# A retention projection by seven block products in place of eight, with its gate's columns ahead of it

## The chip, the cores and the metric

The kernel runs on one core of one Trainium2 chip. The metric is the device time of one execution in microseconds (us); lower is better. A core has five engines that run side by side: TensorE (PE, matmuls into PSUM banks), VectorE (DVE), ScalarE (ACT), GpSimd (POOL, which also issues some transfers) and SyncE (SP, which issues most transfers). Transfers (DMA) run on 16 shared DMA engines.

## The reference

One inference step of a hybrid backbone with one layer, on 128 context tokens and 512 latent tokens. In the part that matters here, the normalised input `h` goes through an input projection; attention gives `ya`, retention gives `yr`, each is projected to 1024 channels, gated, summed and projected again:

```python
def token_mixer(h, ...):
    z = h @ w_in
    q, k, v, rq, rk, rv, rg, ga, gr = jnp.split(z, ...)
    ...
    ya = attend_blocks(q, k_all, v_all)
    yr, s_f, s_b = retention_branch(rq, rk, rv, rg, ...)
    y = jax.nn.sigmoid(ga) * (ya @ w_att_o) + jax.nn.sigmoid(gr) * (yr @ w_ret_o)
    return y @ w_out, (k, v, s_f, s_b)
```

Then come a gated residual add, a second modulated norm, a gated MLP with a width-3 convolution, a second residual add and a last norm. All matrices are float32; `w_ret_o` is 1024 x 1024.

## The kernel before, in words

All 640 tokens (context first, then latent) are handled together, in `NT` = 5 tiles of 128 or in two halves of `HALF` = 320. The 1024 channels are `KD` = 8 rows of 128.

Every float32 matmul operand is split into a high part (a rounding to the type fp32r) and a low part (the rest), and a product is three matmuls: high x high, high x low, low x high. ScalarE makes the high part of a weight by a cast, VectorE the low part by a subtraction (`load_w`, `w_split`). In some places the low part is made by a negated copy on ScalarE and an accumulating transfer that POOL issues. Raw weights come in loads of 1 MB into one of two `raw` buffers; split weights lie in eight `wh` slots of 1024 columns.

There are two matmul helpers. `b_col` makes one column of 128 output channels, transposed (channels on partitions, tokens along the row): for each token half a PSUM bank takes 8 k x 3 matmuls of 128x320, then an evacuation function is called. `a_group` makes 512 output channels for five token tiles, with the activations as the stationary operand: a first round over channels rows 0 to 3 for all tiles, then rows 4 to 7.

The stages around the change, in order:

1. Attention. Its gate columns (`ga`) are left as tanh values in eight tiles `tha` of pool `f1`.
2. The attention projection (`w_att_o`, eight `b_col`); `ya_ev` (L786) multiplies each column with its gate in place. Rows of the modulation matrix `w_mod` are loaded and used in between (`mod_rest`, L254).
3. Retention, whose outputs lie in `rvv` (pool `f0`).
4. The retention projection. `yr_blocks` transposes `rvv` by TensorE into `yrT`, high and low part (L992, L643, L644). `gr_col` makes a column of the retention gate (tanh, L1004), `ret_col` a column of `yr @ w_ret_o`, whose evacuation multiplies by the gate (L1014), adds `tha` (L1015) and splits the sum (`yhi` by ScalarE, L1018; `ylo` by POOL, L1019). Two gate columns come first, beside the transposes; then retention and gate columns alternate.
5. `gate_rows` (L272, L274) spreads the residual gate over the partitions, in tile `gb`.
6. The output projection: `a_group` over the first 512 columns of `w_out` with `evac_out` (L1076 to L1078), then the other 512 tile by tile (`out_half`), followed two tiles behind by `h2_trans`, which writes the second norm's transposed output, split, into `h2`. The buffers of `h2` held the first norm's output `hT` until the last gate column had read it. `h2` has a zero column between context and latent tokens and at the end, for the convolution.
7. The MLP. Its up-projection, but for the first columns, already goes by units of seven block products (`unit_group`, L1343 to L1414): two output columns of 128 by two token halves with the 1024 channels in two halves would be eight block products; sums of weight blocks and of activation blocks make it seven (Strassen's scheme in Winograd's form), each of 4 k x 3 matmuls (L1384 to L1387).

Outside blocks marked `tc.manual_schedule` a planner orders the instructions of each engine before the run, by estimated times; inside a marked block the named engines keep the order of the program. Each engine and each queue then works strictly in its order. A tile that takes the place of a closed pool's tile waits until the last reader of that one is done.

Of the kernel before, what the change touches and what calls it, by code (L numbers as in the profile page):

```python
# [69 lines left out]
def hybrid_step(ctx: ExitStack, tc: tile.TileContext, a: dict, o: dict):  # L70
# [708 lines left out]

    for c in range(KD):  # L780
# [199 lines left out]
    gbp = Pool("gate", side="right")  # L980
    gb = gbp([P, 2, DM])
    yrp = Pool("yr", side="right")
    yrT = [yrp([P, KD, TOK], F32R) for _ in range(2)]
    yrTk = [[x[:, k] for k in range(KD)] for x in yrT]
    rt = Pool("rt", side="right")

# [10 lines left out]
    thr = {}  # L997

    def gr_col(c, w):
        thr[c] = rt([P, TOK], tag="thr", bufs=2)  # L1000
        cc = slice((c % 2) * P, (c % 2 + 1) * P)

        def ev(hf, ts, ps):
            nc.scalar.activation(thr[c][:, ts], ps, AF.Tanh, scale=0.5)  # L1004
        yield from b_col(w, cc, hTk, mm, ev)

    yhi, ylo = {}, {}

    def ret_col(c, w):
        cc = slice((c % 2) * P, (c % 2 + 1) * P)  # L1010

        def ev(hf, ts, ps):
            v = thr[c][:, ts]
            V.scalar_tensor_tensor(v, v, 1.0, ps, op0=ALU.add, op1=ALU.mult)  # L1014
            V.tensor_add(v, v, tha[c][:, ts])  # L1015
            if hf:
                yhi[c] = f1(F32R)
                nc.scalar.copy(yhi[c], thr[c])  # L1018
                nc.gpsimd.tensor_sub(ylo[c], thr[c], yhi[c].bitcast(F32))  # L1019
        yield from b_col(w, cc, yrTk, mm, ev)  # L1020

    def wgr(c):
        return load_w(w_in[:, O_GR + c * P:O_GR + (c + 2) * P], 8, 256)

    yb = yr_blocks()
    wg = wgr(0)
    for c in range(2):
        for _ in gr_col(c, wg):
            next(yb, None)
    run(yb)  # L1030
    ylo4 = [f0(F32R) for _ in range(2)]
    ylo = {c: ylo4[c // 4][:, c % 4] for c in range(KD)}
    for c in range(0, KD, 2):
        wr = load_w(a["w_ret_o"][0, :, c * P:(c + 2) * P], 8, 256)
        if c + 2 < KD:
            wg = wgr(c + 2)
        for j in range(2):
            run(ret_col(c + j, wr))
            if c + 2 < KD:
                run(gr_col(c + 2 + j, wg))  # L1040
# [549 lines left out]
```

## Time and profile before

| | |
|---|---|
| median of 3 runs | 1184.67 us (1184.38 to 1185.37) |
| the profiled execution's own time | 1184.71 us |
| its span in the profile | 1182.9 us |
| granted TensorE clock | 0.998 |
| busy: TensorE / VectorE / ScalarE / POOL | 1153.6 / 738.3 / 567.1 / 175.9 us |
| moved by DMA | 139.02 MB, mean 118 GB/s |

The profile comes from one execution. Its page gives the busy time of each engine, the chain of work that ended last, and groups of instructions by line. Queries of the trace give single instructions in order of time ("start, duration, engine, line, operation, output<-inputs, shapes"), the busy time of each engine in a stretch ("stretch, length, PE busy (count) PEld busy (count) DVE ACT POOL, granted clock, DMA share, GB/s"), and transfers with their size and the time from issue to landing. Matmuls are pipelined: the time from one start to the next is what a matmul costs, not its listed duration.

### The profile page before, as it was taken

Reading aid. Unit: us, or ns where it says so; the run is one execution under the profiler, and the core shown is the slowest. Engines: PE = TensorE matmul, PEld = TensorE weight load, DVE = VectorE, ACT = ScalarE, POOL = GpSimd, SP = SyncE. Lnnn points to the kernel's source line nnn. Section 1 sums busy time; section 2 is a strip of 40 time slices with the busy share of each in tenths; the row PEclk is TensorE's granted clock in tenths of the full one; section 3 lists DMA queues with packets and bytes.
Section 4 is the critical chain, followed back from the end, with each engine's and each line's share of the span. In section 5 each row is a group of like instructions: output and inputs, shape, how many; then the busy total and the mean of one; then the engine's idle time right before and its main releaser. Section 6 shows DMA issues by size and latency. Waiting matters only on the chain.

```text
span 1182.9 us, 18329 instructions
## 1 busy us (share of the span) xinstructions
PE 1153.6 (98%) x7317; PEld 1038.8 (88%) x7317; DVE 738.3 (62%) x1419; ACT 567.1 (48%) x1019; POOL 175.9 (15%) x177
## 2 busy tenths in 40 slices
PE   4999999999999999999999999999999999999996
PEld 4788899999988888888999988999989999899995
DVE  4566977665234436453333339969767688598887
ACT  4355656552132224443222335558657556565473
POOL 0042200000012100033011122011112111121113
PEclk9999999999999999999999999999999999999999
DMA  8742111115554431112122539445666657556543
GB/s 283 250 145 71 37 36 37 36 46 171 213 187 171 153 98 45 36 37 71 36 72 72 180 109 167 111 91 107 158 134 130 142 137 172 125 112 149 141 112 120
DMA packets 130917, 139.02 MB, mean 118 GB/s; under 512 B 26240, under 2 KB 98000, under 8 KB 130832
## 3 DMA queue, kind: packets, MB, share of 16 engines
q1 hardware_dynamic: 106592, 112.95, 29.4%
q0 software_dynamic: 24240, 24.91, 13.8%
q8 instruction: 57, 0.93, 0.3%
q14 instruction: 28, 0.23, 0.1%
HBM read 110.32 MB, written 6.03 MB: 98 GB/s over the span
## 4 chain that ended last, share of the span: by engine, by line
PE 88%; DVE 4%; issue 3%; DMA 2%; POOL 1%; ACT 1%; SPq 0%; DVEq 0%; POOLq 0%; ACTq 0%
DMA t7.u5.5_6930<-in_conv_w 1%; POOL x1.u1.1_6376 L1077 1%; POOL f0.s.5_3520 L941 0%; DVE acts.u2.2_97 L1105 0%; DMA xin.u1.1_108<-in_x_sample 0%; DMA x1.u1.1_6376<-in_x_prompt 0%; DVE acts.u1.1_96 L1104 0%; DVE acts.u2.2_97 L412 0%; PE mm1.mm.11_300 L159 0%; PE mm7.mm.9_7496 L1387 0%; PE mm7.mm.45_9650 L1384 0%; PE mm7.mm.33_8918 L1384 0%; PE mm7.mm.57_10402 L1384 0%; PE mm7.mm.54_10133 L1384 0%; PE mm7.mm.42_9401 L1384 0%
## 5 line engine op out<-in xcount | busy, mean ns | idle before, releaser
L830 POOL TENSOR_TENSOR ret.r2k.6_3630<-ret.u5.5_3523,ret.u1.1_3516 128x256 f32<-128x256 f32 x2 | 1.4, 740 | 205.0 <-ACT ret.u5.5_3523 L826 205.0
L1398 DVE TENSOR_TENSOR t7.u4.4_6925<-t7.u4.4_6925,const.u1.1_70 128x322 f32<-128x322 f32 x10 | 5.0, 496 | 11.6 <-ACT const.u1.1_70 L1397 11.6
L879 DVE SCALAR_TENSOR_TENSOR ret2.u1.1_4317<-ret2.u1.1_4317,const.u13.13_93 64x128 f32<-64x128 f32 x24 | 6.8, 339 | 6.6 <-ACT ret2.u1.1_4317 L872 6.5
L150 DVE TENSOR_TENSOR weights.wh.183_6565<-weights.raw.181_6562,weights.wh.182_6564 128x1024 fp32r<-128x1024 f32 x1 | 1.2, 1224 | 14.3 <-ACT weights.wh.182_6564 L145 14.3
L1309 POOL TENSOR_TENSOR x1.u1.1_6376<-x1.u1.1_6376,weights.raw.410_10987 128x512 f32<-128x512 f32 x5 | 8.2, 1637 | 10.3 <-ACT x1.tm.112_11000 L1281 7.5
L881 DVE SCALAR_TENSOR_TENSOR ret2.u1.1_4317<-ret2.u1.1_4317,const.u13.13_93 64x128 f32<-64x128 f32 x24 | 6.6, 383 | 4.8 <-ACT ret2.u1.1_4317 L874 4.8
L832 DVE TENSOR_TENSOR ret.u5.5_3523<-ret.u5.5_3523,ret.u1.1_3516 128x512 f32<-128x512 f32 x5 | 3.5, 692 | 9.4 <-POOL ret.r2k.8_3701 L830 3.3
L832 DVE TENSOR_TENSOR ret.u4.4_3522<-ret.u4.4_3522,ret.u1.1_3516 128x512 f32<-128x512 f32 x5 | 3.5, 693 | 9.0 <-POOL ret.r2k.11_3881 L830 4.7
L409 ACT CAST acts.u1.1_96<-f0.s.1_109 128x640 fp32r<-128x640 f32 x4 | 2.9, 727 | 11.2 <-DVE f0.s.1_109 L407 11.2
L562 POOL TENSOR_TENSOR p1.u1.1_609<-p1.u3.3_613,p1q.u1.1_603 128x512 f32<-128x512 f32 x1 | 1.3, 1310 | 45.6 <-DMA p1.vc.6_618<-in_cache_v 45.6
L409 ACT CAST acts.u1.1_96<-f0.s.2_110 128x640 fp32r<-128x640 f32 x4 | 2.9, 729 | 10.1 <-DVE f0.s.2_110 L407 10.1
L371 PE MATMUL mm1.mm.1_167<-const.u1.1_70,xin.u1.1_108 128*128 128x128 f32 x4 | 1.1, 435 | 6.8 <-DVE xin.u1.1_108 L362 6.8
L150 DVE TENSOR_TENSOR weights.wh.108_4347<-weights.raw.106_4344,weights.wh.107_4346 128x1024 fp32r<-128x1024 f32 x1 | 1.2, 1226 | 10.3 <-ACT weights.wh.107_4346 L145 10.3
L145 ACT CAST weights.wh.112_4502<-weights.raw.111_4500 128x1024 fp32r<-128x1024 f32 x1 | 1.1, 1050 | 13.3 <-PE mm3.mm.36_4215 L158 13.3
L941 POOL TENSOR_TENSOR f0.s.5_3520<-f0.s.5_3520,ret2.ny20.11_4899 128x512 f32<-128x512 f32 x5 | 6.0, 1235 | 9.1 <-DVE ret2.ny20.11_4899 L217 9.1
L868 POOL DMA_DIRECT2D out_new_state_ret_fwd<-ret.r2k.25_4340 x1 | 0.7, 676 | 43.8 <-ACT ret.r2k.25_4340 L867 43.8
L531 ACT ACTIVATE f0.s.3_715<-f0.s.3_715,p1q.ny20.11_883 128x128 f32<-128x128 f32 x20 | 6.0, 388 | 2.5 <-DVE p1q.ny20.11_883 L215 2.5
L257 DVE COPY mod2.wr.9_4307<-aux3.aux.15_4274 128x128 f32<-128x128 f32 x1 | 0.3, 291 | 10.9 <-PE aux3.aux.15_4274 L254 10.9
L371 PEld LDWEIGHTS mm1.mm.1_167<-const.u1.1_70,xin.u1.1_108 128*128 128x128 f32 x4 | 0.7, 217 | 7.0 <-DVE xin.u1.1_108 L362 7.0
L1275 DVE TENSOR_TENSOR x1.u1.1_6376<-x1.u1.1_6376,gate.u1.1_5306 128x512 f32<-128x512 f32 x10 | 6.8, 685 | 0.0
L145 ACT CAST weights.wh.182_6564<-weights.raw.181_6562 128x1024 fp32r<-128x1024 f32 x1 | 1.1, 1055 | 11.5 <-PE mm3.mm.83_6396 L158 11.5
L145 ACT CAST weights.wh.77_3609<-weights.raw.76_3607 128x1024 fp32r<-128x1024 f32 x1 | 1.0, 1045 | 11.5 <-PE mm3.mm.16_3447 L193 11.5
(7028 smaller groups left out, 4881.6 us busy)
## 6 DMA issues: line engine op xcount, KB each, us to landing
spill.u1.1_6384<-x1.u1.1_6376 POOLq DMA_DIRECT2D x5, 512.0 KB, 4.3
xin.u1.1_108<-in_x_sample SPq DMA_DIRECT2D x4, 512.0 KB
p0.u5.5_125<-in_w_mod SPq DMA_DIRECT2D x2, 1024.0 KB
p0.u6.6_131<-in_w_mod SPq DMA_DIRECT2D x2, 1024.0 KB
p0.u7.7_134<-in_w_mod SPq DMA_DIRECT2D x2, 1024.0 KB
mod.wm.6_2916<-in_w_mod SPq DMA_DIRECT2D x1, 2048.0 KB
mod.wm.8_3067<-in_w_mod SPq DMA_DIRECT2D x1, 2048.0 KB
mod.wm.10_3222<-in_w_mod SPq DMA_DIRECT2D x1, 2048.0 KB
```

Of the source, the lines that this page charges most:

```text
L145: nc.scalar.copy(hi, rv)
L150: (lo_eng or V).tensor_sub(lo, rv, hi.bitcast(F32))
L409: nc.scalar.copy(hT[0][:, k, :], xk)
L531: nc.scalar.activation(x[:, j], x[:, j], AF.Copy, scale=rstd[:, j:j + 1])
L832: V.tensor_mul(z, z, r1[:, t, 0:1, :].to_broadcast([P, 8, 64]))
L879: V.scalar_tensor_tensor(Ss[0:64, hh, st + 1, j], Ss[0:64, hh, st, j], cdsel[0:64, h:h + 1], Ss[0:64, hh, st + 1, j], op0=ALU.mult, op1=AL ...
L881: V.scalar_tensor_tensor(Ss[64:128, hh, 2 - st, j], Ss[64:128, hh, 3 - st, j], cdsel[64:128, h:h + 1], Ss[64:128, hh, 2 - st, j], op0=ALU. ...
L941: nc.gpsimd.tensor_mul(ov, ov, rso[:, 4 * t:4 * t + 4].unsqueeze(2).to_broadcast([P, 4, P]))
L1077: (V if g else nc.gpsimd).tensor_add(x1[:, t, gs], x1[:, t, gs], tm)
L1275: V.tensor_mul(x1[:, t, gs], x1[:, t, gs], gb[:, t == 0, gs])
L1309: eng.tensor_mul(x, x, fg[:, c0:c0 + 512])
L1398: V.tensor_sub(u[1][:, hi_u], u[1][:, hi_u], u3[i])
```

## The change

The retention projection takes the form that the MLP's up-projection has. In detail:

- All eight gate columns come first and stay in one tile `thr` of 8 x 640. The transposes of `yr_blocks` go two to a step beside them.
- `ret_sums` makes three sums of activation blocks and a fourth kept as a product operand, each split; its scratch is the part of `thr` that belongs to columns 6 and 7.
- Four units (`ret_unit`), each for two output columns, do seven products of 4 k x 3 matmuls of 128x320. `prep` makes the weight sums and their split; in two of the seven the low part comes by an accumulating transfer. The products keep the program's order on TensorE; the last product of a unit is done two products into the next.
- Each finished column is multiplied by its gate, and the attention branch's column is added by an accumulating transfer from DRAM. For that, `ya_ev` has written each column of `tha` to DRAM (`thd`).
- The merged column is split straight into `h2`, with the layout of the second norm (a gap after the context tokens), so `a_group` and `out_half` read it with an offset of one for the latent tokens.
- `gate_rows` follows the last product in the same ordered block, and `gb` is allocated after the retention operands are released.

```diff
-    def a_group(w, act, mm, evac, lo_eng=None):
+    def a_group(w, act, mm, evac, lo_eng=None, gap=0):
...
-                ts = slice(t * P, (t + 1) * P)
+                ts = slice(t * P + gap * (t > 0), (t + 1) * P + gap * (t > 0))
...
+    x1d = dp([P, NT, DM])
+    thd = dp([P, KD, TOK])
...
             V.scalar_tensor_tensor(tha[c][:, ts], tha[c][:, ts], 1.0, ps, op0=ALU.add, op1=ALU.mult)
+            if hf:
+                nc.gpsimd.dma_start(thd[:, c, :], tha[c])
...
+    thr = rt([P, KD, TOK])
...
+    def ret_sums():
...
+        x = thr[:, 6:8, :].rearrange("p a b -> p (a b)").rearrange("p (k t) -> p k t", k=4)
...
+        def diff(xs, zs):
+            V.tensor_sub(x, xs[0], zs[0])
+            V.tensor_add(x, x, xs[1])
+            V.tensor_sub(x, x, zs[1])
+
+        def neg_sum(zs):
+            V.scalar_tensor_tensor(x, x, -1.0, zs[0], op0=ALU.mult, op1=ALU.subtract)
+            V.tensor_sub(x, x, zs[1])
+
+        for m, fn in ((3, lambda: diff(q[0, 0], q[1, 0])), (1, lambda: diff(q[1, 1], q[1, 0])),
+                      (2, lambda: neg_sum(q[0, 0])), (4, lambda: neg_sum(q[0, 1]))):
+            fn()
+            nc.scalar.copy(ys[m][0], x)
+            V.tensor_sub(ys[m][1], x, ys[m][0].bitcast(F32))
+
+    for c in range(KD):
...
+        def gr_ev(hf, ts, ps, c=c):
+            nc.scalar.activation(thr[:, c, ts], ps, AF.Tanh, scale=0.5)
+        for _ in b_col(wg, slice((c % 2) * P, (c % 2 + 1) * P), hTk, mm, gr_ev):
+            for _ in range(2):
+                next(yb, None)
+        if c == 1:
+            run(yb)
+            ret_sums()
+
+    def ret_unit(p):
...
+        def prep(m):
+            at, add = PLAN[m]
+            src = bs[at]
+            if add:
+                V.tensor_add(src, src, bs[add])
+            t_ = wp([P, 1024], F32R, tag="wh", bufs=8)
...
+            nc.scalar.copy(hi, src)
+            if m in (2, 3):
+                nc.scalar.activation(lo, src, AF.Copy, scale=-1.0)
+                nc.gpsimd.dma_start(lo, src, accum_op=ALU.add)
+            else:
+                V.tensor_sub(lo, src, hi.bitcast(F32))
...
+        def col(f):
+            c = 2 * p + f
+            V.scalar_tensor_tensor(u[f], thr[:, c, :], 1.0, u[f], op0=ALU.add, op1=ALU.mult)
+            nc.gpsimd.dma_start(u[f], thd[:, c, :], accum_op=ALU.add)
+            for s_, d_ in ((slice(0, P), slice(0, P)), (slice(P, TOK), slice(P + 1, TOK + 1))):
+                nc.scalar.copy(h2[0][:, c, d_], u[f][:, s_])
+                V.tensor_sub(h2[1][:, c, d_], u[f][:, s_], h2[0][:, c, d_].bitcast(F32))
+
+        def prod(m):
...
+            if m == 1:
+                nc.scalar.copy(u[0][:, los], ps)
+            elif m == 5:
+                nc.scalar.activation(u[1][:, his], ps, AF.Copy, scale=-1.0)
+            elif m == 6:
+                nc.scalar.activation(u[1][:, los], ps, AF.Copy, scale=-1.0)
+            elif m == 2:
+                V.tensor_add(u[0][:, los], u[0][:, los], ps)
+            elif m == 7:
+                nc.scalar.copy(u[0][:, his], ps)
+                V.tensor_sub(u[1][:, his], u[1][:, his], u[0][:, his])
+                later.append(lambda: col(1))
+            elif m == 4:
+                nc.scalar.copy(u[0][:, his], ps)
+                later.append(lambda: col(0))
+            else:
+                V.tensor_sub(u[1][:, los], u[1][:, los], ps)
...
+    order = (1, 5, 6, 2, 3, 7, 4)
...
+    with tc.manual_schedule(engines={ET.PE}):
+        ret_pump(0)
+        for n, (p, m) in enumerate(seq):
+            units[p][2](m)
+            ret_pump(n + 1)
+            if later:
+                later.pop(0)()
+        for fn in later:
+            fn()
+        rt.close()
+        yrp.close()
+        gbp = Pool("gate", side="right")
+        gb = gbp([P, 2, DM])
+        gate_rows(0, gb, aux, "aux")
...
-    yk = [[yhi[k] for k in range(KD)], [ylo[k] for k in range(KD)]]
+    yk = [[h[:, k] for k in range(KD)] for h in h2]
...
-    run(a_group(w_out[:, :512], yk, mm, evac_out(0)))
+    run(a_group(w_out[:, :512], yk, mm, evac_out(0), gap=1))
...
-            ts = slice(t * P, (t + 1) * P)
+            ts = slice(t * P + (t > 0), (t + 1) * P + (t > 0))
```

`ret_pump` loads a unit's weights (at most one unit ahead) and prepares products as long as fewer than eight prepared ones are waiting.

More of the change, by code (lines that the diff above doesn't have):

```diff
@@ L995, in yr_blocks @@
                 yield
[L997 to L1020, printed above, removed]
@@ new lines, in hybrid_step @@
+    later = []
+    units = [ret_unit(p) for p in range(KD // 2)]
+    order = (1, 5, 6, 2, 3, 7, 4)
+    preps = [(p, m) for p in range(KD // 2) for m in order]
+    seq, held = [], []
+    for p in range(KD // 2):
+        for m in order[:-1]:
+            seq.append((p, m))
+            held = [(n - 1, y) for n, y in held]
+            if held and held[0][0] == 0:
+                seq.append(held.pop(0)[1])
+        held.append((2, (p, 4)))
+    seq += [y for _, y in held]
+    done, live = 0, []
```

72 lines of the change are left out of this document (47 added, 25 removed).

## The prediction

> **What bounds the kernel now.** First the page, for who is busy; then the busy time by stretch around the place of the change; then the matmul engine's timeline, for its pace; then single lines for the price of each helper; last the transfers.
>
> ```profile
> span 1182.9 us, 18329 instructions
> PE 1153.6 (98%) x7317; PEld 1038.8 (88%) x7317; DVE 738.3 (62%) x1419; ACT 567.1 (48%) x1019; POOL 175.9 (15%) x177
> PE 88%; DVE 4%; issue 3%; DMA 2%; POOL 1%; ACT 1%; SPq 0%; DVEq 0%; POOLq 0%; ACTq 0%
> 571.77:670.50 98.73, 98.73 (x675) 98.73 (x674) 32.36 (x47) 25.32 (x36) 11.43 (x7) 1.00 0.23 75
> 670.50:674.00 3.50, 3.50 (x35) 3.50 (x33) 2.64 (x5) 3.32 (x5) 1.12 (x1) 1.00 0.60 192
> 674.00:687.70 13.70, 13.70 (x63) 11.34 (x62) 0.28 (x1) 1.65 (x3) 0.56 (x1) 1.00 0.55 219
> 887.50:925.00 37.50, 37.50 (x249) 36.82 (x248) 30.66 (x55) 27.17 (x47) 7.12 (x7) 1.00 0.74 157
> 666.83 0.31 PE L194 MATMUL mm3.mm.77_6290<-yr.u1.1_5310,weights.wh.170_6230 128*128 128x320 f32 x1
> 666.98 0.31 PE L192 MATMUL mm3.mm.78_6317<-yr.u1.1_5310,weights.wh.167_6225 128*128 128x320 f32 x1
> 670.50 1.05 PE L272 MATMUL aux3.aux.87_6347<-const.u1.1_70,const.u5.5_85 128*128 128x128 f32 x8
> 667.25 0.49 DVE L1014 SCALAR_TENSOR_TENSOR rt.thr.8_6170<-rt.thr.8_6170,mm3.mm.77_6290 128x320 f32<-128x320 f32 x1 [2.58 <-PE mm3.mm.77_6290 L194]
> ```
>
> TensorE holds 88% of the chain that ended last. In 571.77 to 670.50, the stretch of the retention columns and most of their gate columns, it is busy for all 98.73 us at granted clock 1.00, while VectorE works 32.36 us and ScalarE 25.32. So time goes only if matmuls go, and comes back only if a helper is late. From 666.98 to 670.50 one half column runs: 24 matmuls of 128x320 in 3.52 us, 146.7 ns each.
>
> The profiled execution took 1184.71 us, its span 1182.9; the median of three runs is 1184.67. I sum against 1184.71; 0.04 us between them is nothing. About 0.2% (2.4 us) is what a measurement of this kernel tells from no change.
>
> **The matmuls.** Before: 8 columns x 2 halves x 8 k x 3 = 384. After: 4 units x 7 products x 4 k x 3 = 336, of the same width. The 48 that go are worth 48 x 0.1467 = 7.04 us. Gate columns, transposes and gate rows keep their counts. That seven-product units run at this pace shows later in this kernel:
>
> ```profile
> 898.88 0.31 PE L1384 MATMUL mm7.mm.28_8555<-sums.u1.1_6913,weights.wh.267_8407 128*128 128x322 f32 x1
> 900.64 0.31 PE L1384 MATMUL mm7.mm.24_8418<-acts.u1.1_96,weights.wh.268_8433 128*128 128x322 f32 x1
> ```
>
> One product of 12 matmuls, 322 wide, takes 1.76 us, 146.7 ns per matmul; and the row 887.50 to 925.00, made of such units, is 37.50 of 37.50 busy with VectorE at 30.66 and ScalarE at 27.17. I take 1.76 us a product, 12.3 a unit.
>
> The Trainium skill (TensorE: Matmul & The Clock Gate, Back-to-back issue gap) gives N/2.4 + 2.5 ns for an isolated matmul, 135.8 ns here, and by it the 48 would be worth 6.5 us; its sustained figures, 81 ns at 128 columns and 131 at 512, would put 320 near 107 ns, an estimate, and the gain at 5.1. The trace contradicts both with 146.7 and decides.
>
> **The helpers inside the units.** Their prices:
>
> ```profile
> L1362 DVE TENSOR_TENSOR weights.raw.203_7301<-weights.raw.203_7301 x4: 683/685/692, 771.6 to 782.7; 128x512 f32<-128x512 f32 x4
> L1370 DVE TENSOR_TENSOR weights.wh.281_8647<-weights.raw.269_8436,weights.wh.281_8647 128x512 fp32r<-128x512 f32 x1 | 0.7, 693 | 0.0
> L1395 DVE TENSOR_TENSOR t7.u2.2_6923<-t7.u2.2_6923,mm7.mm.29_8614 128x322 f32<-128x322 f32 x1 | 0.5, 482 | 0.0
> L1186 DVE SCALAR_TENSOR_TENSOR x1.row.63_7605<-t7.tg.8_7680,x1.row.63_7605 128x641 f32<-128x641 f32 x1 | 0.8, 822 | 0.0
> 907.92 0.62 ACT L1365 CAST weights.wh.281_8647<-weights.raw.269_8436 128x512 fp32r<-128x512 f32 x1 [0.62 <-PE mm7.mm.28_8555 L1387]
> L1389 ACT COPY t7.u2.2_6923<-mm7.mm.9_7496 x1: 416/416/416, 790.0 to 790.0; 128x322 f32<-128x322 f32 x1
> 696.09 1.25 ACT L1136 CAST gt.gt0.3_6584<-weights.raw.191_6582 128x1280 fp32r<-128x1280 f32 x1
> 671.59 0.59 ACT L274 COPY gate.u1.1_5306<-aux3.aux.87_6347 128x512 f32<-128x512 f32 x1
> L150 DVE TENSOR_TENSOR weights.wh.153_5756<-weights.raw.151_5753,weights.wh.152_5755 128x1024 fp32r<-128x1024 f32 x1 | 1.2, 1224 | 3.8 <-ACT weights.wh.152_5755 L145 3.8
> L1215 DVE TENSOR_TENSOR gt.gt0.5_7255<-acts.u1.1_96 x2: 1495/1495/1495, 746.4 to 757.7; 128x1288 f32<-128x1288 f32 x2
> weights.wh.237_7878<-weights.raw.227_7704 POOLq DMA_DIRECT2D x1, 256.0 KB, 4.3
> weights.wh.238_7896<-weights.raw.227_7704 POOLq DMA_DIRECT2D x1, 256.0 KB, 5.2
> weights.wh.202_7297<-weights.raw.197_7287 POOLq DMA_DIRECT2D x1, 512.0 KB, 9.0
> ```
>
> VectorE per unit: four weight sums (2.74 us), five low parts (3.45), three bank reads or half subtractions of 320 (1.47), and for each of two columns one gate multiply of 640 (0.82), low parts of 512 (0.69) and 128 (0.3, on the slope between 322 and 512): 3.6. Together 11.3 of 12.3 us. ScalarE: nine casts (5.6), five bank copies (2.1), column copies of 512 and 128 (0.59 and, on the same slope, 0.25; 1.7 for two columns): 9.4. Both fit, VectorE barely. It starts with a lead: four of the eight weight slots come free when gate column 5 is done, so four products (7.0 us of matmuls) can be prepared beside gate columns 6 and 7. The fifth needs an accumulating transfer: its slot comes free 1.8 us before the gate columns end, two casts (1.25), hand-overs (0.3) and 5.2 from issue to landing follow, so it is ready 5.0 us after them, wanted at 7.0. Cost taken: nothing. Gone with the old columns are 16 gate multiplies, 16 adds, eight casts and eight subtractions on POOL, all under TensorE.
>
> In steady order no bank is read and rewritten back to back: a unit's last product is held two products into the next unit. At the very end nothing is left to slip between products 7 and 4 of the last unit, both in one bank. The row at 666.83 plus its 0.31 ends at 667.14 and VectorE follows at 667.25: 0.11 to hand over, 0.42 of copy, about 0.1 back, against a normal step of 0.147 from the last matmul's start: 0.31 + 0.11 + 0.42 + 0.1 - 0.15 = **0.8 us** lost, once.
>
> **The sums of activations** (14 VectorE passes of 1280 columns at 1.5 us, 21 us, and four casts of about 1.25 between) run in the time of gate columns 2 to 7, 42 us. Their scratch lies in rows 6 and 7 of the gate tile, first written about 50 us into the stage (4.3 of transposes, six columns of 7.04, half a column); the sums start near 13, with the last transposed block, and end near 40. Cost: nothing; without that cover up to 26 us.
>
> **The gate columns first.** SP's queue then brings four gate loads and four w_ret_o loads of 1 MB instead of alternating; the DMA share of the stretch is 0.23, so the order costs nothing. Transposes go two per step instead of one; they need the last retention gates, finished within a few us of the stage's start, and the eight gate columns stand in for any wait.
>
> **The spill and its return.** Eight writes of 320 KB go on POOL's queue during the attention projection. There a w_mod load competes:
>
> ```profile
> 294.39 0.37 SPq L246 DMA_DIRECT2D mod.wm.10_3222<-in_w_mod  x1
> 304.00:306.00 2.00, 2.00 (x16) 2.00 (x15) 0.09 (x1) 0.00 (x0) 0.00 (x0) 1.00 0.20 74
> 308.77 0.32 PE L254 MATMUL aux3.aux.5_3306<-mod.wm.10_3222,mod.s128.5_2913 128*32 128x128 f32 x4
> 670.73 0.34 SPq L1067 DMA_DIRECT2D x1.u1.1_6376<-in_x_prompt  x1
> 673.19 0.38 SPq L134 DMA_DIRECT2D weights.raw.186_6572<-in_w_out  x1
> ```
>
> The load goes quiet about 304.5 and is used at 308.77: 4.3 us of slack against one or two spills of under 1 us each. Nothing. The return, an accumulate into the column, lands after about 4.3 us where it is quiet; ScalarE's two copies and VectorE's two subtractions wait for it. Behind them in their queues stand casts and low parts for products to come, which have the lead. So nothing, if the queues are filled with that delay in mind; that is the main doubt (rival A).
>
> **The tail.** Gate rows now follow the last product as before, 3.50 us, then the output projection's first half, 13.70: the two last columns are needed 17.2 us after product 4. Copy 0.42, multiply 0.82, landing 4.3, copies 0.85, subtractions 1.0: 7.4. The x loads, which wait for the retention operands as they did at 670.73, start then too; at the busy row's 9.0 us of landing it is 12.1. Hidden. The Trainium skill (DMA: Bandwidth & Descriptors, Issuing engines are not separate DMA queues) says POOL's and SP's transfers share 16 engines, which speaks against this change just here; the rows 4.3 (256 KB, quiet) and 9.0 (512 KB, busy) agree in kind. By it the end would move only past a landing of 14 us. The output activations in the norm's buffer are overwritten one token tile at a time, two tiles behind their reader: no new wait.
>
> **Sum:** 1184.71 - 7.04 + 0.8 = 1178.5 us.
>
> **Rivals.**
> A, slower: the column copies stand early in ScalarE's and VectorE's queues and hold them until the accumulate lands. With a wait of w per column, VectorE's unit is 11.3 + 2w against 12.3; over four units TensorE loses 8w - 4.0 (its spare) - 7.0 (the lead). It eats the 6.2 us gain from w = 2.1 us on; at a full 4.3 it costs 23.4, and the time is 1202. For it: nothing before made these two engines wait for an accumulate, and VectorE has 8% spare. Against: the waits fall beside products prepared ahead, and back-to-back VectorE passes start closer together than their durations. At w = 2.1 to 2.7: 1185 to 1189.
>
> B, no change: the low parts of gate columns 4 and 5 queue behind the activation sums on VectorE. If they come only after all of them, at about 40 us of the stage where TensorE wants them at 32.5, 7 us go: 1185.5. Against: the casts between the sums leave gaps of 1.25 us, and a low part of 1024 columns takes 1.2.
>
> C, the change saves less than it says: bank copies come late inside the units. Each is read by ScalarE while one product of another bank runs, 1.76 us; a copy (0.42) that finds two casts ahead of it (1.24) and two hand-overs is late by about 0.1. On each of 28 turns that makes 2.8 us: 1181.3.
>
> **Chances.** Forecast 0.52, C 0.16 (both faster: 0.68). Within 0.2%: B 0.07 and A at w near 2.1, 0.09: 0.16. Slower: A beyond, 0.16. The likeliest case alone spans 1177 (no bank wait, a little won at other waits) to 1180. The range reaches from 1176.5 to 1189, A at w = 2.7; beyond it A keeps about 0.12.
>
> **What would show it.** 48 fewer matmuls; the retention products at 1.76 us each; TensorE full from the first gate column to the gate rows but for one gap near 0.8 us before the last product. A: ScalarE's wait list names the DMA of the column tile, TensorE waits for low parts of weights in units 1 to 3. B: TensorE waits in gate columns 4 or 5. C: many waits of tenths of a us for ScalarE copies. The prediction is wrong if TensorE's idle time between the gate columns and the gate rows is above 3 us, or if the stretch after the gate rows lengthens.

## The result and the profile after

The change made the kernel slower: 1203.59 us (median of four runs, 1203.30 to 1203.98) against 1185.02 us (1184.38 to 1185.56), a ratio of 1.0157 with a 95% interval of 1.0140 to 1.0175. The forecast was 1178.5.

First the page of the kernel after, its span and its busy times:

```profile
span 1202.2 us, 18413 instructions
PE 1157.1 (96%) x7269; PEld 1037.2 (86%) x7269; DVE 775.2 (64%) x1465; ACT 591.2 (49%) x1079; POOL 184.4 (15%) x193
```

48 matmuls fewer (7269 against 7317), as predicted, and yet 19.3 us more span, of which 3.5 us is TensorE's busy time. So TensorE waited, and some of its matmuls were slower. To find where, the span is cut at the same instructions in both traces: the first gate column, the gate rows, the output projection's second half, the first matmul of the up projection. Busy time by stretch (length, PE busy (count), PEld, DVE, ACT, POOL, granted clock, DMA share, GB/s), before:

```profile
553.34:670.50 117.16, 117.16 (x809) 117.01 (x808) 41.48 (x58) 34.37 (x50) 12.90 (x9) 1.00 0.22 73
670.50:701.32 30.82, 30.82 (x154) 26.10 (x153) 11.06 (x14) 11.13 (x17) 5.78 (x5) 1.00 0.42 154
701.32:731.11 29.79, 29.79 (x145) 24.92 (x144) 22.67 (x76) 12.01 (x26) 6.66 (x11) 1.00 0.87 156
```

and after:

```profile
553.30:679.80 126.50, 115.68 (x764) 113.79 (x763) 77.18 (x100) 57.78 (x107) 17.17 (x16) 0.96 0.45 99
679.80:710.59 30.79, 30.79 (x152) 25.57 (x150) 9.32 (x14) 7.77 (x15) 5.78 (x9) 1.00 0.88 146
710.59:751.14 40.55, 35.29 (x146) 27.37 (x144) 26.59 (x80) 16.07 (x31) 6.89 (x8) 0.87 0.42 140
```

There are two losses, in two places. The retention stage takes 126.50 us in place of 117.16, though it has 48 matmuls less. The output projection's second half takes 40.55 in place of 29.79, and the change touches its work only in where it reads its activations. The stretch between them takes as long as before. In both bad stretches TensorE is not busy throughout, and its granted clock is below 1.00. TensorE's waits in this window, longest first (engine, what waited, its line, whom for: us, times, longest):

```profile
PE mm3.mm.69_6166 L1086 <- ACT f1.s.14_5877 L1095: 4.9, 1, 4.9
PE mm3.mm.80_6677 L157 <- ACT weights.wh.199_6655 L145: 3.1, 1, 3.1
PE mm3.mm.72_6300 L1086 <- ACT f1.s.16_5879 L1095: 3.0, 1, 3.0
PE mm3.mm.72_6300 L1086 <- ACT f1.s.15_5878 L1099: 2.4, 1, 2.4
PE mm3.mm.80_6677 L158 <- DVE weights.wh.200_6656 L150: 1.3, 1, 1.3
```

Four of the five name ScalarE. Lines 1095 and 1099 are bank copies inside the units (they empty a PSUM bank so that its next product can start; 0.4 us of work each), line 145 is the cast of w_out's second half. Why such a short copy was late is read from ScalarE's own timeline, with the transfer that POOL issued and the product that waited:

```profile
642.57 0.45 ACT L1093 ACTIVATE f1.s.14_5877<-mm3.mm.70_6183 128x320 f32<-128x320 f32 x1
643.35 0.89 POOL L1075 DMA_DIRECT2D f1.s.12_5875<-spill.u2.2_2893  x1 [4.41 <-DVE f1.s.12_5875 L1074]
645.02 0.62 ACT L1062 CAST weights.wh.177_6198<-weights.raw.168_6024 128x512 fp32r<-128x512 f32 x1 [2.00 <-DVE weights.raw.168_6024 L1059]
650.34 0.82 ACT L1077 CAST acts.u1.1_96<-f1.s.12_5875 128x128 fp32r<-128x128 f32 x2 [4.70 <-DMA f1.s.12_5875<-spill.u2.2_2893]
653.04 0.43 ACT L1095 ACTIVATE f1.s.14_5877<-mm3.mm.69_6166 128x320 f32<-128x320 f32 x1
653.53 0.63 PE L1086 MATMUL mm3.mm.69_6166<-rt.u2.2_5510,weights.wh.174_6139 128*128 128x320 f32 x1 [4.87 <-ACT f1.s.14_5877 L1095]
653.96 0.47 PE L1088 MATMUL mm3.mm.69_6166<-rt.u3.3_5511,weights.wh.174_6139 128*128 128x320 f32 x1
654.22 0.47 PE L1089 MATMUL mm3.mm.69_6166<-rt.u2.2_5510,weights.wh.174_6139 128*128 128x320 f32 x1
```

This is rival A. POOL issues the return of an attention column at 643.35; ScalarE stands idle for 4.70 us at the column copies (L1077) until it has landed, 7.0 us after its issue. The bank copy of L1095 stands behind them in the queue and comes at 653.04, so the next product of that bank starts at 653.53, after 4.87 us without work. All eight columns do this; ScalarE's idle times before L1077 are 1.8 to 7.1 us.

The last two rows show a second price: after the wait the matmuls stand 0.26 us apart in place of 0.147. Busy time by stretch across that wait:

```profile
648.00:654.00 6.00, 1.13 (x7) 0.87 (x6) 3.07 (x6) 2.62 (x7) 0.48 (x1) 0.85 0.38 106
654.00:660.00 6.00, 6.00 (x27) 6.00 (x27) 2.56 (x6) 3.29 (x8) 2.99 (x3) 0.58 0.94 122
```

The granted clock is 0.58 in the 6 us that follow. The Trainium skill (TensorE: Matmul & The Clock Gate, Part 1: The HAM clock gate) says that the array's clock is halved after an idle window of about 3.4 us and comes back after about 3.4 us of work. The trace agrees in kind: 320 columns at half of the Trainium skill's 2.4 GHz are 0.267 us, an estimate, against the 0.26 here. In length it differs: the clock stays at 0.50 for 5.5 us of work (653.50 to 659.00), and in a run below (`pin3_conv_late`) it falls to 0.57 behind a wait of only 2.94 us:

```profile
652.00:656.00 4.00, 4.00 (x19) 4.00 (x18) 1.27 (x3) 1.15 (x3) 2.61 (x2) 0.57 0.96 129
```

The second loss is on SP's queue. SP's timeline after (first seven rows, the loads; then ScalarE's cast of the w_up load and the cast of w_out behind it):

```profile
681.93 0.37 SPq L134 DMA_DIRECT2D weights.raw.198_6653<-in_w_out  x1
682.39 2.31 SPq L1174 DMA_DIRECT2D x1.u1.1_6460<-in_x_prompt  x1
684.75 2.07 SPq L1174 DMA_DIRECT2D x1.u1.1_6460<-in_x_sample  x4
686.86 15.05 SPq L1263 DMA_DIRECT2D t7.u5.5_7011<-in_conv_w  x3
701.95 3.67 SPq L1264 DMA_DIRECT2D t7.u5.5_7011<-in_conv_b  x1
705.72 3.48 SPq L134 DMA_DIRECT2D weights.raw.203_6663<-in_w_up  x1
715.88 1.26 ACT L1243 CAST gt.gt0.3_6665<-weights.raw.203_6663 128x1280 fp32r<-128x1280 f32 x1 [10.63 <-DMA weights.raw.203_6663<-in_w_up]
718.40 1.03 ACT L145 CAST weights.wh.199_6655<-weights.raw.198_6653 128x1024 fp32r<-128x1024 f32 x1
```

Before, SP's timeline had these loads in another order:

```profile
690.04 0.38 SPq L134 DMA_DIRECT2D weights.raw.191_6582<-in_w_up  x1
706.80 10.80 SPq L1156 DMA_DIRECT2D t7.u5.5_6930<-in_conv_w  x3
717.65 5.02 SPq L1157 DMA_DIRECT2D t7.u5.5_6930<-in_conv_b  x1
```

The four loads of the convolution's parameters, 22 KB each, hold SP's queue for 18.7 us. Before, they came behind the w_up loads. After, they stand ahead of the first one, which goes out at 705.72, 4.9 us ahead of the output projection's second half (710.59) where it had been 11.3. ScalarE waits 10.63 us for it, and the cast of w_out, for which TensorE waits 3.1 us, stands behind that wait. Why they are issued earlier is not settled. One trace of it is the clearing of `ub`, tiles allocated just ahead of theirs (POOL, before, after, and in a run below, `eight_conv_late`, that puts the activations in the norm's buffer but has neither units nor returns):

```profile
730.06 0.43 POOL L1151 MEMSET t7.u1.1_6922<- 128x1 f32 x1
```

```profile
683.47 0.43 POOL L1258 MEMSET t7.u1.1_7003<- 128x1 f32 x1
```

```profile
644.14 0.10 POOL L1140 MEMSET t7.u1.1_6922<- 128x1 f32 x1 [86.51 <-DVE rt.u1.1_5319 L1022]
```

This fits memory that belonged to the output activations before (`yhi`, `ylo` in `f1` and `f0`) and comes free earlier once they lie in the norm's buffer. But it does not date the loads themselves: before, they went out at 706.80, 23 us ahead of that clearing. That the freed memory is the reason is therefore an inference; no run moves the activations alone and leaves the loads to the planner.

### The profile page after: what moved, and what is told of

It reads as the page before. It is cut to its first block, busy times and chain, and to the rows that moved or that the text cites. A ratio compares the mean times of both kernels' runs of the same rounds, so it can differ in the third digit from the quotient of the medians.

```text
span 1202.2 us, 18413 instructions
## 1 busy us (share of the span) xinstructions
PE 1157.1 (96%) x7269; PEld 1037.2 (86%) x7269; DVE 775.2 (64%) x1465; ACT 591.2 (49%) x1079; POOL 184.4 (15%) x193
## 4 chain that ended last, share of the span: by engine, by line
PE 41%; issue 6%; DVE 3%; DMA 1%; POOL 1%; ACT 1%; DVEq 0%; POOLq 0%; ACTq 0%
DMA x1.u1.1_6460<-in_x_prompt 1%; DMA f1.s.14_5877<-spill.u2.2_2893 1%; POOL x1.u1.1_6460 L1184 1%; DVE acts.u2.2_97 L1212 0%; DVE acts.u1.1_96 L1211 0%; DVE x1.u1.1_6460 L1184 0%; ACT x1.u1.1_6460 L1376 0%; PE mm7.mm.9_7577 L1494 0%; PE mm7.mm.45_9731 L1491 0%; PE mm7.mm.21_8267 L1491 0%; PE mm7.mm.57_10483 L1491 0%; PE mm7.mm.30_8750 L1491 0%; PE mm7.mm.33_8999 L1491 0%; PE mm7.mm.63_10849 L1493 0%; PE mm7.mm.33_8999 L1494 0%
## 5 line engine op out<-in xcount | busy, mean ns | idle before, releaser
L1416 POOL TENSOR_TENSOR x1.u1.1_6460<-x1.u1.1_6460,weights.raw.422_11068 128x512 f32<-128x512 f32 x5 | 8.2, 1641 | 10.3 <-ACT x1.tm.112_11081 L1388 7.4
L150 DVE TENSOR_TENSOR weights.wh.108_4359<-weights.raw.106_4356,weights.wh.107_4358 128x1024 fp32r<-128x1024 f32 x1 | 1.2, 1225 | 10.3 <-ACT weights.wh.107_4358 L145 10.3
```

The costliest lines, as they stand in the source:

```text
L1416: eng.tensor_mul(x, x, fg[:, c0:c0 + 512])
```

## The experiments

All ratios are to the kernel before, timed again beside each of three groups of runs (1184.59, 1185.34 and 1184.84 us), with 95% intervals; a difference between runs of two groups can be off by the 0.75 us between these. The diffs are shortened. In every run the stages before the change, and those from the up projection on, are the same work.

### Each loss alone, and both

`conv_late` emits the four loads after the first load of w_up's gate half and pins them behind it in SP's queue. (That is the second w_up load; the expectations say the third, which is where they stood in the kernel before.)

```diff
     w_g = load_w(w_up[:, FF:FF + 256], 8, 256, "dma")
+    with tc.issue_after(last_w):            # last_w: the load just traced
+        for i in range(3):
+            nc.sync.dma_start(cw[:, i, :], a["conv_w"]...)
+        nc.sync.dma_start(cw[:, 3, :], a["conv_b"]...)
```

> The kernel after, with one thing moved: the four loads of the convolution's parameters stand in SP's queue behind the third load of w_up (as in the kernel before) in place of ahead of the first. Theory (two separate losses, this is the second): the loads hold the queue for 18.7 us, the first w_up load goes out at 705.7 in place of about 687, its cast stands in ScalarE's queue ahead of the casts of w_out's second half, and TensorE loses 10.7 us in the output projection's second half; so the stretch from its first matmul to the first of the up projection falls from 40.5 us to about 30 and the time from 1203.6 to about 1193. The waits of the retention units stay at about 10.6 us. Rival (w_out's halves are late because their weight slots come free late after the disturbed units, and the place of the small loads does not matter): the stretch stays near 40 and the time at 1202 to 1204.

1194.67 us, ratio 1.0090 (1.0075 to 1.0106): 8.9 us won. The second half of the output projection takes 30.47 us, with no wait; TensorE's waits in the units stay at 10.8 us. The theory of the second loss holds; its size is 1.8 us under the expected 10.7.

`no_return` takes out the accumulating transfer:

```diff
-            nc.gpsimd.dma_start(u[f], thd[:, c, :], accum_op=ALU.add)
```

> The kernel after without the accumulating transfer that adds the attention branch to each column, so the output lacks that branch; all else, the spill too, stays. Theory (first loss): ScalarE's and VectorE's column steps wait for that transfer and hold the bank copies behind them; without it the stretch from the first gate matmul to the output projection's second half falls from 157.3 us by about 15 to about 142, TensorE's waits in the units from 10.6 us to under 1, the time from 1203.6 to about 1188. Rival (VectorE at 11.3 us of each unit's 12.3 is simply too slow, or the helpers' sums are): TensorE's waits in the units stay above 8 us and the time above 1200.

1182.73 us, ratio 0.9986 (0.9976 to 0.9995): 20.9 us won, 5 more than the first loss is worth. The units' waits are gone, so VectorE is not too slow and the rival falls. (Without the return the output lacks the attention branch; the run serves for its time alone.) The surplus is in the second loss, and SP's timelines show how. Without the returns, and (from a run below) with them but with nobody waiting:

```profile
669.59 14.17 SPq L1262 DMA_DIRECT2D t7.u5.5_7003<-in_conv_w  x3
687.51 3.65 SPq L134 DMA_DIRECT2D weights.raw.203_6655<-in_w_up  x1
```

```profile
670.87 17.20 SPq L1274 DMA_DIRECT2D t7.u5.5_7011<-in_conv_w  x3
691.99 3.42 SPq L134 DMA_DIRECT2D weights.raw.203_6663<-in_w_up  x1
```

With the returns in flight the three loads start 1.3 us later and hold the queue 3.0 us longer, so w_up goes out 4.5 us later.

`no_return_conv_late` has both edits.

> Both edits: no accumulating transfer (the attention branch is left out of the output) and the convolution's loads behind the third w_up load. Theory: the two losses are separate and add, 15.5 + 10.7, and what is left is the change as forecast: 1203.6 - 26.2 = 1177.4, between 1177 and 1180. Rival (they overlap, the first loss makes part of the second): about 1183 to 1188 and nothing more than the larger of the two alone.

1179.32 us, ratio 0.9954 (0.9939 to 0.9969). With both away the kernel is within 1 us of the forecast. The sum of the two single gains (29.8) is more than the gain of both (24.3); the 5.5 us are the part of the second loss that the returns make. So the expectation that the two add is refuted, though the time fell in its range.

### Keep the return, move its waiters

`pin6_conv_late` computes everything. The column's copies and subtractions are emitted six products later and pinned behind the bank reads traced by then; the multiply and the transfer stay where they were:

```diff
             nc.gpsimd.dma_start(u[f], thd[:, c, :], accum_op=ALU.add)
-            for s_, d_ in (...):
-                nc.scalar.copy(h2[0][:, c, d_], u[f][:, s_])
-                V.tensor_sub(h2[1][:, c, d_], ...)
+            back.append([6, lambda: put(f)])          # counted down once per product
+
+        def put(f):
+            c = 2 * p + f
+            with tc.issue_after(last_a), tc.issue_after(last_v):   # last bank reads of ScalarE, VectorE
+                for s_, d_ in (...):
+                    nc.scalar.copy(h2[0][:, c, d_], u[f][:, s_])
+                    V.tensor_sub(h2[1][:, c, d_], ...)
```

> All of the computation. The convolution's loads behind the third w_up load, and each column's two copies and two subtractions are put in ScalarE's and VectorE's queues behind the bank reads of the product six places later, some 10 us after the transfer is issued, in place of right behind the gate multiply. Theory (the transfer costs nothing in itself, only what stands behind its waiters does): TensorE waits in the units under 2 us in all, time 1178 to 1182, faster than the kernel before by 0.3 to 0.6%. Rival (the accumulating transfer itself is the cost: it lands 7 us and more after its issue where a 1 MB load runs beside it, and its load on the DMA engines delays the low parts too): waits of 4 us or more stay in the units and the time is 1184 to 1193.

1179.51 us, ratio 0.9956 (0.9939 to 0.9973): the change as it was meant, 5.1 us faster than the kernel before. Its busy time by stretch, for the units and the first gate columns:

```profile
552.00:612.00 60.00, 59.80 (x413) 59.14 (x412) 40.18 (x39) 25.74 (x42) 3.93 (x3) 1.00 0.21 58
612.00:640.00 28.00, 28.00 (x193) 28.00 (x192) 18.97 (x31) 17.48 (x36) 8.21 (x7) 1.00 0.76 143
640.00:680.00 40.00, 40.00 (x251) 37.50 (x250) 24.04 (x41) 20.55 (x42) 8.03 (x12) 1.00 0.91 231
```

TensorE is busy for all of 68 us, with the returns running (DMA share 0.76 and 0.91) and the same work on VectorE and ScalarE. The transfer costs nothing where nothing needed soon stands behind its waiters.

Three more distances, with the convolution's loads late in all of them: the 6 of the diff becomes 2, 3 and 4.

> The convolution's loads behind the third w_up load, and the column steps pinned behind the bank reads only two products later, some 3.5 us after the transfer is issued, where the landings were 4.2 to 7.2 us. Theory (the loss is landing time minus distance in the queue, once the prepared lead is used up): a part of the waits comes back, ScalarE waits 1 to 4 us before several column copies, TensorE loses 1 to 6 us in the units, time 1181 to 1186, between 1179.5 (six products) and 1194.7 (none). Rival (any place behind the next bank reads is enough): no waits over 0.5 us on TensorE and 1179.5.

> As the run with the column steps two products later, but three. For the odd columns this puts ScalarE's two copies 1.8 us further back, behind one more bank read; the even columns stand where they stood. Theory (TensorE's loss is the landing time minus the distance that the queue gives, and the copies of the odd columns, which held it for 4.9 and 3.2 us, make most of it): the two waits shrink by about 1.8 us each, TensorE's waits in the units go from 10.3 to 5 to 7 us, and the time from 1194.9 to 1187 to 1190. Rival (a threshold: any bank read ahead of the copies frees TensorE): under 1183.

> As before, four products later: the odd columns' copies another 1.8 us back, the even columns' behind one more bank read. Theory: distances of about 6 to 7 us against landings of 4.2 to 7.2; TensorE's waits in the units fall under 2 us and the time to 1180 to 1182. Rival (the transfers themselves slow the unit, whatever stands behind them): above 1183.

TensorE's waits in the units, and the time:

| products later | waits, us | time, us | ratio and interval |
|---|---|---|---|
| as in the change | 10.8 | 1194.67 | 1.0090 (1.0075 to 1.0106) |
| 2 | 10.3 | 1194.87 | 1.0091 (1.0077 to 1.0105) |
| 3 | 6.7 | 1189.51 | 1.0040 (1.0027 to 1.0054) |
| 4 | 0 | 1179.66 | 0.9957 (0.9943 to 0.9971) |
| 6 | 0 | 1179.51 | 0.9956 (0.9939 to 0.9973) |

The run with two missed its expectation: nothing came back. Its ScalarE queue shows why: the copies stand almost where the planner had put them by itself, which would fit a planner that reckons with a landing of about two products, 3.5 us (an inference). From there on each product more puts the odd columns' copies 1.8 us further back, and the waits go from 10.3 to 6.7 and to none. Wait by wait the expectation for three holds less well than in the sum: the longest falls from 4.9 to 2.9, the second grows from 3.2 to 3.8, and the two smaller ones (1.7 and 0.5) vanish. TensorE's waits with three:

```profile
PE mm3.mm.72_6296 L1093 <- ACT f1.s.16_5879 L1102: 3.8, 1, 3.8
PE mm3.mm.69_6162 L1093 <- ACT f1.s.14_5877 L1102: 2.9, 1, 2.9
```

Between none and the full loss, 10.8 us of waits cost 15.2 us of time and 6.7 cost 10.0: every waited us costs 1.4 to 1.5, the excess being the slow clock behind it. In the second loss it is more: 8.9 us for 5.3 us of waits in the kernel after, 9.0 for 5.0 in `pin6` below, 1.7 to 1.8 a us, since there short waits follow one another while the clock is at 0.50.

### What makes the second loss

> The column steps six products later as in the run with both edits, and the convolution's loads left ahead of the first w_up load. Theory (the second loss is a matter of how late the w_up load goes out against the output projection's second half, and the disturbed units made most of that lateness): as without the return, the load goes out some 8 us ahead of that half where 11.6 are needed, and 3.4 us are lost: 1179.5 + 3.4 = 1182.9, faster than before by 0.1 to 0.2%. Rivals: the two losses are independent, 10.7 stay and the time is about 1190; or the conv loads cost nothing once the units are in order, 1179.5.

`pin6` is the run with six products and the loads left ahead of w_up: 1188.51 us, ratio 1.0030 (1.0018 to 1.0041). It missed: 9.0 us are lost, not 3.4. So the second loss does not come from the disturbed units. With the gain from 1203.59 (15.1) this splits the loss, and in either order alike (8.9 and 15.2 with the loads moved first): 15.1 for the waiters, 9.0 for the loads (8.8 by the ratios).

This is the old kernel with the loads ahead of w_up:

```diff
+    cw = cp([P, 4, 2 * NF])
...
+    with tc.issue_after(last_x):
+        for i in range(3):
+            nc.sync.dma_start(cw[:, i, :], a["conv_w"]...)
+        last_cw = nc.sync.dma_start(cw[:, 3, :], a["conv_b"]...)
+    with tc.issue_after(last_cw):
         raw = w_raw(w_up[:, :256], 8, 256)
```

> The kernel before, with one thing of the kernel after put into it: the convolution's four loads stand in SP's queue behind the x loads and the last w_out load and ahead of the first w_up load (their tile lies in the constants' buffer, which is free at that time). Theory (SP's queue alone makes the second loss, and only by how late the w_up load goes out): the loads hold the queue from about 673.6 to 692.3, so the w_up load goes out some 2.3 us later than at 690.04; TensorE then waits up to 2.5 us in the output projection's second half, behind the cast of w_up: 1186 to 1187.5. Rival (the loads cost time only together with something else of the change, such as its x loads or its later evictions): 1184.6.

1184.09 us, ratio 0.9991 (0.9982 to 0.9999): no loss in the time, so the expected 1186 to 1187.5 is refuted. In the trace the stage does lose: TensorE waits 0.8 us there, and from the second half to the up projection it takes 30.97 us against 29.79. The span has 1.5 us less behind that; TensorE's lag of 1.26 us at 712 shrinks step by step to a lead of 0.34 at 1122, like a difference in pace. The edit also moves `cw` to another place in memory, which may be the reason; the run does not separate the two. The load goes out only 1 us later than before, as issued 691.10 against 690.04.

Over these runs the loss follows one number, the time of the w_up cast on ScalarE against the start of the output projection's second half, because two casts of w_out stand behind it. It starts 5.4 us ahead of that point in `pin6_conv_late` (no wait), 1.6 ahead in `before_conv_early` (0.8 us), 0.5 behind in `no_return` (2.2), 5.0 behind in `pin6` (5.0) and 5.3 behind in the kernel after (5.3). ScalarE's row in `pin6`:

```profile
701.30 1.26 ACT L1254 CAST gt.gt0.3_6665<-weights.raw.203_6663 128x1280 fp32r<-128x1280 f32 x1 [10.38 <-DMA weights.raw.203_6663<-in_w_up]
```

### The products by themselves

`eight_conv_late` keeps the new order, the norm's buffer and the late loads, but makes the columns by the old helper and adds the attention branch from SBUF:

```diff
+    for c in range(KD):
+        if c % 2 == 0:
+            wr = load_w(a["w_ret_o"][0, :, c * P:(c + 2) * P], 8, 256)
+        run(ret_col(c, wr))       # b_col; gate, tensor_add of tha[c], split into h2
```

> The change without its core: gate columns first, output in the norm's buffer, the convolution's loads behind the third w_up load, but eight block products (the old 24 matmuls of each half column), no sums of activations, no spill and no return, the attention branch added from SBUF by VectorE. Theory (the 48 matmuls are worth 48 x 0.1467 = 7.0 us, and the rest of the change is neutral): 1179.5 + 7.0 = 1186.5 if what the run with both edits lost against the forecast (1 us) lies in the units, and 1184.6 to 1185.5 if in the reordering nothing is lost. Rival (part of the gain came from the new order, not from the products): below 1183.

1186.11 us, ratio 1.0009 (1.0000 to 1.0017). From the first gate column to the output projection's second half, eight products and then seven:

```profile
553.20:702.17 148.97, 148.76 (x962) 143.14 (x960) 60.15 (x87) 47.06 (x75) 5.87 (x10) 1.00 0.26 89
554.05:696.04 141.99, 141.78 (x913) 135.94 (x912) 90.76 (x117) 69.82 (x127) 23.27 (x26) 1.00 0.52 127
```

The 48 matmuls are worth 6.98 us, and the time differs by 6.6 (6.3 by the ratios). The gain lies in the products; the order is not the source of it, and costs about 1 us of its own (148.97 against 117.16 + 30.82 = 147.98 before).

### The pace of the output projection

That 1 us is mostly pace. Four times the same 108 matmuls of 128x512, the last of the first half: in the kernel before, with the old kernel's high parts shifted by 4 bytes (and all tiles of their pool made 64 bytes longer for it), in `pin6_conv_late`, and with the rows of the norm's buffer padded so that every piece begins on a multiple of 64 bytes.

```diff
-    hflat = [hp([P, KD * 2 * HW], F32R) for _ in range(2)]
+    hflat = [hp([P, KD * 656], F32R) for _ in range(2)]     # aligned: rows 656 apart
...
-            for s_, d_ in ((slice(0, P), slice(0, P)), (slice(P, TOK), slice(P + 1, TOK + 1))):
+            for s_, d_ in ((slice(0, P), slice(0, P)), (slice(P, TOK), slice(P + 16, TOK + 16))):
```

```diff
-        return f1p([P, TOK], dtype, tag="s", bufs=8)
+        return f1p([P, TOK + 16], dtype, tag="s", bufs=8)[:, :TOK]     # before_shift
...
-                yhi[c] = f1(F32R)
+                yhi[c] = f1p([P, TOK + 16], F32R, tag="s", bufs=8)[:, 1:TOK + 1]     # before_shift
```

> The run with the column steps six products later and the convolution's loads behind the third w_up load, and in addition the rows of the norm's buffer are 656 elements apart in place of 644 and the output activations' sample tokens begin at element 144 in place of 129, so that every 128-column piece that the output projection loads as weights starts on a multiple of 64 bytes, as it did in the kernel before. Theory (the output projection's 240 matmuls of 512 columns, 227.5 ns apart in the kernel before and 233.2 ns here, are slower because their stationary pieces start off such a boundary): 227.5 ns again, 240 x 5.7 = 1.4 us less, 1178.1. Rival (they are slower for another reason, such as both operands' place in memory or the two halves now lying in one tile each): 233 ns and 1179.5.

> The kernel before with the high parts of the output activations moved by one element (4 bytes) inside tiles that are 64 bytes longer; nothing else. Theory (stationary pieces off a 64-byte boundary make the output projection's matmuls slower): two of every three of its 240 matmuls have the high part as stationary; they go from 227.5 to about 233 ns, 160 x 5.7 = 0.9 us more, 1185.5 against 1184.6, seen in the matmuls' distances sooner than in the time. Rival: 227.5 ns everywhere and no difference.

```profile
676.84:701.32 24.48, 24.48 (x109) 20.27 (x108) 8.41 (x9) 7.22 (x11) 4.09 (x4) 1.00 0.32 118
```

```profile
677.01:702.09 25.08, 25.08 (x110) 20.27 (x109) 8.54 (x9) 7.22 (x11) 4.24 (x4) 1.00 0.32 117
```

```profile
670.91:696.04 25.13, 25.13 (x109) 20.30 (x108) 10.30 (x13) 9.23 (x16) 4.21 (x4) 1.00 0.53 183
```

```profile
666.78:691.81 25.03, 25.03 (x109) 20.33 (x108) 10.37 (x13) 9.30 (x16) 4.21 (x4) 1.00 0.55 186
```

226.7 ns a matmul before, 232.2 shifted, 232.7 in the new buffer, 231.8 padded. Where the operands lie does set the pace: shifting them slowed the old kernel nearly as much as the new buffer does, and by more than the expectation's two thirds of 5.7 ns (in the time, 1185.78 us, ratio 1.0006, 0.9997 to 1.0015, it does not show). But the 64-byte boundary is not the rule: with it restored the pace did not come back. What about the addresses matters stays open.

`aligned` is nevertheless the fastest kernel of all: 1177.35 us, ratio 0.9936 (0.9924 to 0.9949), faster than the kernel before by 0.5 to 0.8% (the traced execution took 1176.35). It wins in another place than expected: its first gate column starts at 549.46 us where that of `pin6_conv_late` starts at 554.05, so 4.6 us are won ahead of the changed stage; from there on it is 1.2 us slower. Of the 4.6, 1.1 are there after the first 37 us. The rest is again pace: the distance from a 128x512 matmul ahead of that column to the next start is 232.5 ns in place of 239.1 behind low x high (401 of them), 232.3 in place of 235.7 behind high x low (399) and 241.1 in place of 239.5 behind high x high (401), distances over 0.5 us left out; together 3.4 us. TensorE's first matmuls of that column, `aligned` first:

```profile
549.46 0.31 PE L196 MATMUL mm3.mm.47_5334<-acts.u1.1_96,weights.wh.132_5326 128*128 128x320 f32 x1
```

```profile
554.05 0.30 PE L194 MATMUL mm3.mm.47_5334<-acts.u1.1_96,weights.wh.132_5326 128*128 128x320 f32 x1
```

## Why the prediction was wrong, by its own steps

**The matmuls: right.** 48 fewer, at 146.7 ns, 7.04 us forecast; 6.98 us measured between the eight- and seven-product runs, 145 ns each. The pace of units held: in all runs the products that did not wait started 1.76 us apart. The estimate of 135.8 ns from the formula of the Trainium skill (TensorE: Matmul & The Clock Gate, Back-to-back issue gap) would have given 6.5.

**The helpers inside the units: right in its verdict, wrong in size.** Summed durations made VectorE 11.3 and ScalarE 9.4 of 12.3 us. In `pin6_conv_late` they are busy 18.97 and 17.48 us of the first 28 us of units, which is 8.3 and 7.7 of 12.3. Instructions that follow each other directly overlap (ScalarE's casts of 0.62 us start 0.51 apart), so sums of durations overstate the load. There was room, and rival A's "VectorE has 8% spare" was not the reason why A came.

**The return: the step that failed.** The prediction wrote "nothing, if the queues are filled with that delay in mind" and gave the other case 0.25 in all. They were not: moving the waiters four products or more back brought TensorE's waits in the units to none, and two products back, some 3.5 us, changed nothing. In the kernel after the landing took 4.5 to 7.1 us in the units (8.2 for the last column), against the 4.3 that the prediction had read from a quiet row. The first half of rival A is what happened: the column copies stood early in the queues and held them until the transfer had landed. Its price came near, and that is in part luck: with the mean idle time of 3.8 us its formula gives 8 x 3.8 - 11 = 19 us, against 15.1 measured by moving the waiters. The formula put all of it into waiting; in fact 10.6 us are waits and the rest is the slow clock after them. The slot that the prediction named as threatened was also another one: not low parts of weights for later products, but the bank copies, for which no lead exists, since a bank's next product cannot start without them. The lead of four products, subtracted in the formula, protects only the weights.

**The activations in the norm's buffer, "no new wait": the second step that failed.** It asked who reads the buffer and not what else moves in the queues. In the kernel after the convolution's loads come 20 us earlier, into the one place of SP's queue where a late load is felt: 9.0 us, shown by moving them back. That the memory freed by the move let them come is an inference. The step "the gate columns first" had looked at SP's queue for its own eight loads and the tail for the x loads; the four small loads behind those were not followed. The sum had no term for it. The prediction's sign for this ("if the stretch after the gate rows lengthens") was the right one to look at.

**The tail: right.** In the kernel after the last two returns were issued at 681.06 and 682.93 and their copies ran at 686.35 and 691.19, and TensorE was busy throughout from 680 to 712. The transfers share the DMA engines as the Trainium skill says (DMA: Bandwidth & Descriptors, Issuing engines are not separate DMA queues); this case's number for it is the 3.0 us by which the returns lengthened SP's small loads.

**The bank wait of 0.8 us: did not come.** In `pin6_conv_late` three matmuls of the output projection, ready early, fill the place between products 7 and 4 of the last unit. They are not lost time, since the projection then has three fewer.

**The sums of activations, the gate columns first, the spill: right.** No wait over 0.2 us up to the first product. Rivals B and C did not occur.

**What the sum did not have:** 240 matmuls of the output projection at 5.7 ns more, 1.4 us, which fits where the activations lie. With it and the wait of 0.2 us beside the transposes, 1184.6 - 7.0 + 1.4 + 0.2 = 1179.2, against 1179.5 for the change with both losses removed.

## What to carry to other kernels

An instruction that waits for a transfer belongs in its engine's queue as far behind the issue as the transfer takes at its slowest there, here 7 us or four products, and what must be looked up is not how busy that engine is but which short, undelayable copies (bank reads) stand behind it. When a tile moves, look for what now starts earlier (here perhaps because of the memory that it leaves), and follow each queue to the next load that is needed in time: 88 KB of parameters in tiny pieces cost more here than the 48 saved matmuls gained. TensorE's waits of some us cost 1.4 to 1.8 times their length here.

## What the runs showed of the hardware that was not expected

After a wait of 4.87 us the granted clock was 0.58 for the next 6 us, and a wait of 2.94 us lowered it to 0.57 for 4 us. Over whole stages each us of waiting cost 1.4 to 1.5 us in the units and 1.7 to 1.8 in the output projection's second half. Four loads of 22 KB held SP's queue for 18.7 us (13 to 21 in the other runs), 3.0 us longer with other transfers in flight. The pace of a 128x512 matmul depended on where its activations lie, 226.7 to 232.7 ns, and a longer buffer alone made earlier stages 4.6 us shorter; which property of the addresses does this is open.
